# One hybrid decoder step on Trainium2: attention written as 16 steps, with each decode unit's stages apart and three shared banks

## The chip, the cores and the metric

The kernel runs on one core of a Trainium2 chip (trn2). The metric is the device time of one execution in microseconds; the median of the runs counts. On the core, TensorE (PE) multiplies, VectorE (DVE) and ScalarE (ACT) evict and do pointwise work, GpSimd (POOL) does little here, and SyncE (SP) issues the DMAs, in one queue.

## What is computed

```python
x = x + 0.5 * swiglu(rms_norm(x, f1n), f1g, f1u, f1d)
h = rms_norm(x, mix_n)
q, k, v, g, a_low, c_q, c_kv, k_pe_raw = jnp.split(h @ w_in, offsets, axis=-1)
o_gla, S = gla_mix(*gla_inputs(q, k, v, a_low, w_a_up, b_a))
y_gla = gla_output(o_gla, g, g_norm)
q_nope, q_pe, lat, k_pe = mla_project(c_q, c_kv, k_pe_raw, pos, q_norm, kv_norm, w_uq)
y_mla = mla_attend(q_nope, q_pe, lat, k_pe, w_uk, w_uv)
x = x + jnp.concatenate([y_gla, y_mla], axis=-1) @ w_out
x = x + 0.5 * swiglu(rms_norm(x, f2n), f2g, f2u, f2d)
```

There is one prompt of 1024 new tokens and eight samples of one new token each, with 4096 past tokens in a paged cache (latents of 128 and rotary keys of 64 a token). The width is 1024, the FFN's inner width 2816. Attention has four heads. For the prompt it is

```python
s = (jnp.einsum('bqhd,bkhd->bhqk', qn, k_nope)
     + jnp.einsum('bqhr,bkr->bhqk', qp, k_pe)).astype(jnp.float32) * MLA_SCALE
s = jnp.where(kpos[None, :] <= qpos[:, None], s, -jnp.inf)
p = jax.nn.softmax(s, axis=-1)
return jnp.einsum('bqhk,bkhd->bqhd', p.astype(v.dtype), v)
```

and for the samples the same over the cached latents, with the key and value weights absorbed into the queries and the output.

## The kernel before, in words

The program runs FFN1, the input projection, GLA, attention, the output projection with the mixer's sum, FFN2 and the last norm. All large products are three fp32r matmuls over a high and a low part of each operand; `split` (L83) makes the two parts, the high one on ACT (L84), the low one on DVE (L85), and `mm3` (L87, its matmul is L93) issues the three. The order of the instructions on each engine is left to the framework's scheduler, which takes what is ready by the order of the text; the text and the numbers of buffers in the pools are all that sets it.

*Pages.* Before decode can read the cache, 256 pairs of DMAs (`copies`, L188) bring its pages to contiguous DRAM (`kvd`, `ped`). `beside(n)` (L199) issues n of them: one after each of FFN1's seven products (L318, in `seven`), two at each tile of the input projection (L761), the rest ahead of GLA's levels (L1051).

*Decode.* There are 16 units (g, u), each of four samples and 512 past positions. `dec_unit` (L1191) does one in a row: fetch four latent tiles `kvt` and four key tiles `pet`; turn them with fp32 PE transposes, four to a bank (L1202 for `pet`, L1210 for `kvt`), copied to SBUF by DVE (`peT`, L1205) and ACT (`latT`, L1212); scores into one bank `dsc` (L1215, four matmuls of 512 columns, and L1218, eight of 256); softmax (L1188, L1189); four transposes of the probabilities `dpp` (L1224), a copy `dpT` (L1225), and 16 value matmuls (L1229). `dec_combine` adds the samples' own token and joins the eight units of a group. All these banks come from one pool of two, tag `pd` (the scores' bank from the same pool under a second tag).

*Prompt attention.* For each of two pairs of heads: the rotary queries `qs`, the values `v` (L1347 to L1349), then for each head the keys `k`, and four query blocks of 256. A block's `scores` makes the queries `q_h`, `q_l` and the score chunks `sc` (L1387 to L1393, three banks), the maximum, the exponentials `pp` (L1402) and their scaling (L1408). `outputs` of the block before turns `pp` (L1423, four transposes to a bank), splits it into `pT_h`, `pT_l` and multiplies by the values into `po` (one bank). Then `decode(1)` does one unit. Queries, keys, values and pp turns share two banks, tag `ps`. Two units are done ahead, during GLA.

After attention, `project` (from L1477) takes the GLA outputs `yraw`, split into `yg_h`, `yg_l`, the attention outputs `ym_h`, `ym_l`, and w_out (`raw`, split into `wh`, `wl`). The pool `raw` is shared by loads of all stages.

Of the kernel before, what the change touches and what calls it, by code (L numbers as in the profile page):

```python
# [67 lines left out]
def hybrid_step(ctx: ExitStack, tc: tile.TileContext, I, O, C):  # L68
# [226 lines left out]
    def seven(A, todo):  # L295
# [3 lines left out]
        for i in (1, 6, 2, 7, 5, 3, 4):  # L299
# [18 lines left out]
            beside()  # L318
# [517 lines left out]
    def rope(pool_, tag, dst, src, n, s):  # L836

        L = s.stop - s.start
        W = 512 if tag == "pp" else BL
        w = pool_.tile([P, 2 * W], F32, name="ropew", tag=tag, bufs=3 if tag == "pp" else 1)  # L840
# [101 lines left out]
    def levels(qr, st):  # L942
# [108 lines left out]
    beside(len(units) * 16)  # L1051
# [99 lines left out]

    early_raw = []
    for srcs in ([qnd[:, 0]], [qnd[:, 1]], [latd], [kpd, kpd]):
        raw = rawp.tile([P, SEQ], F32, name="raw", tag="raw")
        w = P // len(srcs)
        for i, src in enumerate(srcs):
            ld.dma_start(raw[i * w:(i + 1) * w], src)
# [4 lines left out]
    psD_cm, psd = pool("psD", 2, space=PSUM, side="right")  # L1162

    def dbank(name="pd"):
        return psd.tile([P, 512], F32, name=name, tag="pd")
# [6 lines left out]
    oT = ep.tile([P, NS, 32], F32, name="oT", bufs=1)  # L1172
    uv = ep.tile([P, 4, P], F32, name="uv", bufs=1)
    ld.dma_start(uv, w_uv)
    grp = {}

    def fetch(g, u):

        kvt = [ep.tile([P, J, P], F32, name="kvt", tag="kvt", bufs=6) for _ in range(4)]
        pet = [ep.tile([P, J, 64], F32, name="pet", tag="pet", bufs=6) for _ in range(4)]  # L1180
# [3 lines left out]
        return kvt, pet  # L1184
# [6 lines left out]
    def dec_unit(g, u):  # L1191

        if u == 0:
            grp[g] = (ep.tile([P, 3, NU + 1], F32, name="stat", tag="stat"), ep.tile([P, NU + 1, P], F32, name="oc", tag="oc", bufs=1))
        oc = grp[g][1]
        kvt, pet = fetch(g, u)
        sc = dbank("dsc")
        lt, pe = [], []
        for b2 in range(2):
            p = dbank()  # L1200
            for q in range(4):
                PE.transpose(p[:, q * P:(q + 1) * P],  # L1202
                             pet[2 * b2 + q // 2][:, 2 * (q % 2):2 * (q % 2) + 2, :].rearrange("p j c -> p (j c)"), ident)
            peT = ep.tile([P, 512], F32, name="peT", tag="peT")
            V.tensor_copy(peT, p)  # L1205
            pe += [peT[:, :256], peT[:, 256:]]
        for bi in range(4):
            p = dbank()
            for q in range(4):
                PE.transpose(p[:, q * P:(q + 1) * P], kvt[bi][:, 2 * (q % 2) + q // 2, :], ident)  # L1210
            lt.append(ep.tile([P, 512], F32, name="latT", tag="latT", bufs=4))
            S.activation(lt[bi], p, AF.Copy)  # L1212
        rows = [slice(32 * bi, 32 * bi + 32) for bi in range(4)]
        for bi in range(4):
            PE.matmul(sc[rows[bi], :], qlp[:, 4 * g + bi], lt[bi], start=True, stop=False)  # L1215
        for par in range(2):
            for bi in range(4):
                PE.matmul(sc[rows[bi], par * 256:par * 256 + 256], qpp[par][:, 4 * g + bi], pe[bi], start=False, stop=par == 1)  # L1218
        pp = ep.tile([P, 512], F32, name="dpp", tag="dpp")
        softmax(g, u, sc, 512, pp)  # L1220
        pT = ep.tile([P, J, P], F32, name="dpT", tag="dpT")
        p = dbank()
        for q in range(4):
            PE.transpose(p[:, q * P:(q + 1) * P], pp[:, q * P:(q + 1) * P], ident)  # L1224
        V.tensor_copy(pT.rearrange("p j q -> p (j q)"), p)  # L1225
        po = dbank()
# [3 lines left out]
        V.tensor_copy(oc[:, u], po[:, :P])  # L1230

    def dec_combine(g):
        stat, oc = grp[g]

        p = dbank()
        for bi in range(4):
            b = 4 * g + bi
            PE.matmul(p[32 * bi:32 * bi + 32, :NS], qlp[:, b], lat_s, start=True, stop=False)
            PE.matmul(p[32 * bi:32 * bi + 32, :NS], qpp[0][:64, b], kp_s, start=False, stop=True)
        sn = ep.tile([P, NS], F32, name="sn", tag="sn")  # L1240
        V.tensor_add(sn, p[:, :NS], newmask[:, g * NS:(g + 1) * NS])
        pn = ep.tile([P, NS], F32, name="pn", tag="pn")
        softmax(g, NU, sn, NS, pn)
        p = dbank()
        PE.transpose(p[:NS, :P], pn, ident)
        pnT = ep.tile([NS, P], F32, name="pnT", tag="pnT", bufs=1)
        V.tensor_copy(pnT, p[:NS, :P])
        p = dbank()
# [3 lines left out]
        cm = ep.tile([P, 4], F32, name="cm", tag="cm")  # L1252
        V.tensor_reduce(cm[:, 0:1], stat[:, 0, :], AX.X, OP.min)
        S.activation(stat[:, 2, :], stat[:, 0, :], AF.Exp, bias=cm[:, 0:1], scale=-1.0)
        V.tensor_mul(stat[:, 1, :], stat[:, 1, :], stat[:, 2, :])
        V.tensor_reduce(cm[:, 2:3], stat[:, 1, :], AX.X, OP.add)
        V.reciprocal(cm[:, 3:4], cm[:, 2:3])
        om = ep.tile([P, P], F32, name="om", tag="om", bufs=1)
        V.tensor_scalar_mul(om, oc[:, 0], stat[:, 2, 0:1])
        for u in range(1, NU + 1):  # L1260
            V.scalar_tensor_tensor(om, oc[:, u], stat[:, 2, u:u + 1], om, op0=OP.mult, op1=OP.add)
        V.tensor_scalar_mul(om, om, cm[:, 3:4])
        p = dbank()
# [428 lines left out]
```

## Time and profile before

| | |
|---|---|
| Median of three runs | 2098.72 us |
| Range of the runs | 2098.38 to 2100.55 us |
| Profiled execution, its time | 2100.9 us |
| Its span | 2099.1 us |
| PE busy | 2031.5 us (97%) |
| PE weight loads | 1915.6 us (91%) |
| DVE, ACT busy | 1471.5 us (70%), 838.0 us (40%) |
| Mean granted PE clock | 0.989 |

A row of the timeline gives the start, the duration, the engine and line, the operation with its output and inputs, and in brackets how long the engine was idle just before and what released it. A run of equal instructions is one row. The end of a matmul is modelled: the next one may start before it. "PE" is the matmul and "PEld" the load of its weights. The granted clock is given as a share of full speed, 1.00 being 2.4 GHz and 0.50 being 1.2 GHz.

### The profile page before, as it was taken

Reading aid. Unit: us, or ns where it says so; the run is one execution under the profiler, and the core shown is the slowest. Engines: PE = TensorE matmul, PEld = TensorE weight load, DVE = VectorE, ACT = ScalarE, POOL = GpSimd, SP = SyncE. Lnnn points to the kernel's source line nnn. Section 1 sums busy time; section 2 is a strip of 40 time slices with the busy share of each in tenths; the row PEclk is TensorE's granted clock in tenths of the full one; section 3 lists DMA queues with packets and bytes.
Section 4 is the critical chain, followed back from the end, with each engine's and each line's share of the span. In section 5 each row is a group of like instructions: output and inputs, shape, how many; then the busy total and the mean of one; then the engine's idle time right before and its main releaser. Section 6 shows DMA issues by size and latency. Waiting matters only on the chain.

```text
span 2099.1 us, 42793 instructions
## 1 busy us (share of the span) xinstructions
PE 2031.5 (97%) x16379; PEld 1915.6 (91%) x16379; DVE 1471.5 (70%) x2902; ACT 838.0 (40%) x1563; POOL 64.1 (3%) x95
## 2 busy tenths in 40 slices
PE   9999999999999999889899999999999999999997
PEld 8999999999999988888667777799999999999997
DVE  7876676675777865766565766488777778766775
ACT  7432322233344530436554644244323323333534
POOL 0000000000000000311000000000000000000000
PEclk9999999999999999999999999999999999999999
DMA  6444445467565623012443342744323233574352
GB/s 215 130 144 141 127 126 152 131 203 265 159 187 152 166 75 99 11 42 81 129 129 96 115 128 60 221 136 122 91 92 121 87 88 122 159 260 146 110 158 92
DMA packets 235837, 276.46 MB, mean 132 GB/s; under 512 B 27216, under 2 KB 186128, under 8 KB 235632
## 3 DMA queue, kind: packets, MB, share of 16 engines
q1 hardware_dynamic: 235632, 273.72, 42.7%
q8 instruction: 129, 2.11, 0.4%
q14 instruction: 76, 0.62, 0.1%
HBM read 214.34 MB, written 84.47 MB: 142 GB/s over the span
## 4 chain that ended last, share of the span: by engine, by line
PE 80%; DVE 8%; DMA 3%; ACT 3%; issue 2%; SPq 1%; POOL 1%; POOLq 0%; DVEq 0%; ACTq 0%
PE pp L93 34%; PE pp L448 20%; PE pw L93 6%; PE pr L93 4%; PE po L93 1%; PE pd L1210 1%; PE pw L1076 1%; PE dsc L1215 1%; DVE al L85 1%; PE pg L973 1%; PE ps L93 1%; PE dsc L1218 1%; PE ps L1423 1%; PE pd L1229 1%; DMA kvt<-kvd 1%
## 5 line engine op out<-in xcount | busy, mean ns | idle before, releaser
L93 PE MATMUL pp<-bh,ah 128*128 128x260 f32 (+1 forms) x2432 | 688.3, 283 | 9.7 <-DVE u L310 6.8
L93 PE MATMUL pp<-bl,ah 128*128 128x260 f32 (+1 forms) x2432 | 687.1, 283 | 1.8 <-DVE bl L85 1.8
L93 PE MATMUL pp<-bh,al 128*128 128x260 f32 (+1 forms) x2432 | 687.0, 283 | 0.6 <-DVE al L85 0.6
L93 PEld LDWEIGHTS pp<-bh,ah 128*128 128x128 f32 x2432 | 460.7, 189 | 12.1 <-DVE u L310 7.8
L93 PEld LDWEIGHTS pp<-bh,al 128*128 128x128 f32 x2432 | 462.1, 190 | 1.7 <-DVE al L85 1.7
L93 PEld LDWEIGHTS pp<-bl,ah 128*128 128x128 f32 x2432 | 459.8, 189 | 2.4 <-DVE bl L85 2.4
L448 PE MATMUL pp<-th,dl 128*128 128x256 f32 x1232 | 248.6, 283 | 1.2 <-DVE dl L85 1.2
L448 PE MATMUL pp<-tl,dh 128*128 128x256 f32 x1232 | 248.9, 283 | 0.1
L448 PE MATMUL pp<-th,dh 128*128 128x256 f32 (+1 forms) x1232 | 248.9, 283 | 0.0
L84 ACT ACTIVATE ah<-raw 128x512 fp32r<-128x512 f32 x208 | 128.8, 627 | 236.5 <-PE pp L93 219.0
L448 PEld LDWEIGHTS pp<-tl,dh 128*128 128x128 f32 x1232 | 190.0, 189 | 2.4 <-DVE tl L85 2.4
L448 PEld LDWEIGHTS pp<-th,dl 128*128 128x128 f32 x1232 | 189.9, 188 | 1.4 <-DVE dl L85 1.4
L448 PEld LDWEIGHTS pp<-th,dh 128*128 128x128 f32 x1232 | 190.8, 189 | 0.1
L84 ACT ACTIVATE dh<-a 128x1024 fp32r<-128x1024 f32 (+1 forms) x84 | 83.0, 988 | 253.9 <-PE pp L448 226.5
L85 DVE TENSOR_TENSOR al<-raw,ah 128x512 fp32r<-128x512 f32 x208 | 142.3, 688 | 48.7 <-ACT ah L84 47.2
L85 DVE TENSOR_TENSOR dl<-a,dh 128x1024 fp32r<-128x1024 f32 (+1 forms) x84 | 95.3, 1134 | 114.5 <-ACT dh L84 108.1
L84 ACT ACTIVATE ah<-sl 128x512 fp32r<-128x512 f32 x132 | 82.9, 630 | 201.0 <-PE pp L93 154.0
L93 PE MATMUL pw<-xh,wh 128*128 128x260 f32 (+4 forms) x320 | 101.1, 316 | 0.0
L93 PE MATMUL pw<-xh,wl 128*128 128x260 f32 (+4 forms) x320 | 100.5, 314 | 0.0
L93 PE MATMUL pw<-xl,wh 128*128 128x260 f32 (+4 forms) x320 | 100.1, 313 | 0.0
L85 DVE TENSOR_TENSOR tl<-traw,th 128x1032 fp32r<-128x1032 f32 (+1 forms) x84 | 95.6, 1138 | 3.8 <-ACT th L84 3.6
L85 DVE TENSOR_TENSOR al<-sl,ah 128x512 fp32r<-128x512 f32 x132 | 90.5, 688 | 10.9 <-ACT ah L84 8.1
(426 smaller groups left out, 3571.1 us busy)
## 6 DMA issues: line engine op xcount, KB each, us to landing
traw<-td SPq DMA_DIRECT2D x70, 516.0 KB
raw<-in_ffn_w_gate_dram SPq DMA_DIRECT2D x52, 512.0 KB
raw<-in_ffn_w_up_dram SPq DMA_DIRECT2D x52, 512.0 KB
a<-in_ffn_w_down_dram SPq DMA_DIRECT2D x40, 512.0 KB
kvd<-in_cache_kv_dram SPq DMA_DIRECT2D x256, 64.0 KB
kvt<-kvd SPq DMA_DIRECT2D x64, 256.0 KB
td<-q SPq DMA_DIRECT2D x22, 520.0 KB
td<-q SPq DMA_DIRECT2D x22, 512.0 KB
```

The source lines that it names most:

```text
L84: S.activation(out_h, src, AF.Copy)
L85: eng.tensor_sub(out_l, src, out_h)
L93: PE.matmul(ps, w_, x_, start=i == 0, stop=i == n - 1)
L448: PE.matmul(bank[c][m], w_[:, kk, ms], x_[:, kk, c * N[0]:c * N[0] + N[c]], start=first and j == 0 and (c == 1 or m % 2 == 0), stop=last a ...
L973: PE.matmul(p[:, t, c], kt[:, t, c * P:(c + 1) * P], qt[:, t, :, c * 64:(c + 1) * 64], start=True, stop=True)
L1076: PE.matmul(p[:n, :256], x_[:, k], w_[:, k % 4, :], start=i == 0, stop=i == 3 * KD - 1)
L1210: PE.transpose(p[:, q * P:(q + 1) * P], kvt[bi][:, 2 * (q % 2) + q // 2, :], ident)
L1215: PE.matmul(sc[rows[bi], :], qlp[:, 4 * g + bi], lt[bi], start=True, stop=False)
L1218: PE.matmul(sc[rows[bi], par * 256:par * 256 + 256], qpp[par][:, 4 * g + bi], pe[bi], start=False, stop=par == 1)
L1229: PE.matmul(po[rows[bi], :P], pT[:, (j % 2) * 2 + j // 2, rows[bi]], kvt[bi][:, j], start=j == 0, stop=j == J - 1)
L1423: PE.transpose(p[:, jj, qi * P:(qi + 1) * P], prs[qi][:, (j + jj) * P:(j + jj + 1) * P], ident)
```

## The change

1. Page copies: `seven` issues a copy after three of its seven products, the input projection four at each tile, GLA's `levels` four at each level, and the block of all remaining copies goes.
2. The rotary tables of the input projection's end and of attention come from the pool `raw`.
3. Attention is written as 16 steps, one for each head and block. `dec_unit` is cut into `fetch`, `turn`, `dec_scores`, `dec_softmax`, `dec_turn` and `dec_values`; `dec_own` and `dec_combine` are generators that go on a piece at a time (`tick`). In a step come the scores of the first query tile, the unit's scores, its softmax, the second query tile, the old block's pp turns, the unit's probability turn, the products, the values and the next unit's six turns (`t(0)` to `t(5)`) one at a time between these, and the next block's queries. Tiles are fetched two units ahead.
4. Banks: one for a unit's scores, its probability turns and its values (`sc_`); three, tag `ps`, for the unit's turns, pp turns, queries, keys, values and rotary queries. During GLA each of the two early units has one bank for turns and one for the rest.
5. Buffers: 11 `kvt` and 8 `pet` (6 and 6 before), `pp` as six tiles of 512 columns (three of 1024), `pT` two (three), `dpp`, `dpT` one (two).
6. `first_w`, one buffer of `raw`, is loaded ahead of the query and latent rows with the first heads' weights and the causal mask; `kp` is loaded later, inside attention; the value weights for the samples are loaded at the end, into a buffer of `raw`.

```diff
-            beside()
+            if i in (6, 7, 3):
+                beside()
...
-        beside(2)
+        beside(4)
...
+            beside(4)
...
-    beside(len(units) * 16)
...
+    first_w = rawp.tile([P, 1024], F32, name="first_w", tag="raw")
+    fw3 = [first_w[:, 256 * i:256 * i + 256].rearrange("p (k f) -> p k f", k=2) for i in range(3)]
+    for hh in range(2):
+        ld.dma_start(fw3[0][:, :, 64 * hh:64 * hh + 64], w_uq_[:, :, hh * 192 + P:hh * 192 + 192])
...
+
+    def dbank(tag="pt"):
+        if tag == "sc":
+            return unit_bank.tile([P, 512], F32, name="sc_", tag="sc_", bufs=1)
+        return psd.tile([P, 512], F32, name="pt", tag="ps") if psd is not unit_bank else psd.tile([P, 512], F32, name="pt", tag="pt", bufs=1)
...
+        kvt = [ep.tile([P, J, P], F32, name="kvt", tag="kvt", bufs=11) for _ in range(4)]
+        pet = [ep.tile([P, J, 64], F32, name="pet", tag="pet", bufs=8) for _ in range(4)]
...
+    def turn(g, u, i):
+
+        kvt, pet = got[g, u]
+        p = dbank()
+        for q in range(4):
+            src = kvt[i][:, 2 * (q % 2) + q // 2, :] if i < 4 else \
+                pet[2 * (i - 4) + q // 2][:, 2 * (q % 2):2 * (q % 2) + 2, :].rearrange("p j c -> p (j c)")
+            PE.transpose(p[:, q * P:(q + 1) * P], src, ident)
+        t_ = ep.tile([P, 512], F32, name="latT" if i < 4 else "peT", tag="latT" if i < 4 else "peT", bufs=4 if i < 4 else 2)
+        if i < 4:
+            S.activation(t_, p, AF.Copy)
+        else:
+            V.tensor_copy(t_, p)
+        turned[g, u, i] = t_
...
+    EARLY = 2
...
+    psD_cm, unit_bank = pool("psU", 1, space=PSUM, side="right")
+    ps_cm, ps = pool("psA_", 3, space=PSUM)
+    psd = ps
...
+    load_uqr(0)
+    split(qn_h[:, 0], qn_l[:, 0], early_raw[0])
+    split(qn_h[:, 1], qn_l[:, 1], early_raw[1])
+    rotary(0, 0, loads=True)
+    load_uk(0)
+    split(lat_h, lat_l, early_raw[2])
+    load_uq(0)
+    keys(0, 0)
+    queries(0, 0)
+    load_uv(0)
+    turn(*units[0], 0)
+    kraw_ = rawp.tile([P, SEQ], F32, name="raw", tag="raw")
+    for i in range(2):
+        ld.dma_start(kraw_[64 * i:64 * i + 64], kpd)
+    rotary(0, 0)
+    turn(*units[0], 4)
+    split(kp_h, kp_l, kraw_)
+    V.tensor_copy(identb, ident)
+    V.tensor_copy(causalb, first_w[:, 896:])
+    turn(*units[0], 1)
+    values(0, 0)
+    turn(*units[0], 5)
+    rotary(0, 1, loads=True)
+    values(0, 1)
+    turn(*units[0], 2)
+    turn(*units[0], 3)
+    rotary(0, 1)
...
+        s0 = scores(h, m, 0)
+        d(dec_scores)
+        maximum(*s0)
+        pr0 = exps(*s0, 0)
+        d(dec_softmax)
+        t(0)
+        s1 = scores(h, m, 1)
+        maximum(*s1)
+        factor(*s0)
+        if old:
+            old.turn(0)
+            old.part(0)
+            old.turn(1)
+            old.part(1)
+        pr1 = exps(*s1, 1)
+        tick()
+        t(4)
+        d(dec_turn)
+        if m == 3 and h == 1:
+            rotary(1, 0, loads=True)
+        t(1)
+        if old:
+            old.turn(2)
+            old.product(0)
+            old.part(2)
+        scale(pr0, s0[1])
+        factor(*s1)
+        tick()
+        if i and h % 2 == 0:
+            values(h // 2, 2 * m)
+        if m == 3 and h < 3:
+            load_uk(h + 1)
+            if h != 1:
+                load_uq(h + 1)
+        t(5)
+        if old:
+            old.turn(3)
+            old.product(1)
+            old.part(3)
+        if m == 3 and h == 1:
+            rotary(1, 0)
+        if unit and unit[1] == 0:
+            tick(20)
+        d(dec_values)
+        if new:
+            queries(*new)
+        scale(pr1, s1[1])
+        t(2)
...
+        if old:
+            old.product(2)
...
+        t(3)
+        if old:
+            old.product(3)
+            old.out()
...
+    uv = rawp.tile([P, 4, P], F32, name="uvr", tag="raw")
+    ld.dma_start(uv, w_uv)
+    old.turn(0)
...
```

**PE, a block in the steady part.** `pd<-ident,kvt` are turns of the decode tiles, `dsc` (after: `sc__`) the decode scores, `po` the prompt's value products, `ps<-ident,pp` the probability turns, `sc` the prompt's scores. Before, from the third last product of a block to the first scores of the next unit:

```order
L93 MATMUL po<-pT_l,v_h 128x256
L93 MATMUL po<-pT_h,v_l 128x256
L1210 MATMUL pd<-ident,kvt 128x128 x4
L93 MATMUL ps<-qn_h,uqh 128x256
L93 MATMUL ps<-qn_l,uqh 128x256
L1210 MATMUL pd<-ident,kvt 128x128 x8
L93 MATMUL ps<-qn_h,uql 128x256
L93 MATMUL ps<-qn_h,uqh 128x256
L1210 MATMUL pd<-ident,kvt 128x128 x4
L1215 MATMUL dsc<-latT,qlp 32x512 x4
L1218 MATMUL dsc<-peT,qpp_11185 32x256 x4
L1218 MATMUL dsc<-peT,qpp_11186 32x256 x4
```

The change, one unit's scores and what comes after:

```order
L1228 MATMUL sc__15509<-peT,qpp_10217 32x256 x4
L1228 MATMUL sc__15509<-peT,qpp_10218 32x256 x4
L1204 MATMUL pt<-ident,kvt 128x128 x4
L1452 MATMUL sc<-k_l,q_h 128x512
L1453 MATMUL sc<-k_h,q_l 128x512
L1454 MATMUL sc<-kp_h,qs_15198 128x512
L1455 MATMUL sc<-kp_l,qs_15198 128x512
L1457 LDWEIGHTS identb
L1457 MATMUL sc<-causalb,identb 128x128
L1502 MATMUL ps<-ident,pp 128x128 x4
L1204 MATMUL pt<-ident,pet 128x128 x4
L1239 MATMUL sc__15509<-ident,dpp 128x128 x4
```

Before, the four turns of the `kvt` tiles stand with two or three matmuls between them, right ahead of the scores that read them. After, the scores stand together, and the next unit's first `kvt` turn, a `pet` turn and a pp turn are apart, with the prompt's scores between the decode scores and the turn of their probabilities.

**PE, the front of attention.** Before, from the values of unit 1 on:

```order
L1229 MATMUL pd<-kvt,dpT 32x128 x16
L1202 MATMUL pd<-ident,pet 128x128 x4
L1347 MATMUL ps<-uv_h,lat_h 128x256
L1348 MATMUL ps<-uv_h,lat_l 128x256
L1349 MATMUL ps<-uv_l,lat_h 128x256
L1202 MATMUL pd<-ident,pet 128x128 x4
L1347 MATMUL ps<-uv_h,lat_h 128x256
L1348 MATMUL ps<-uv_h,lat_l 128x256
L1349 MATMUL ps<-uv_l,lat_h 128x256
L1210 MATMUL pd<-ident,kvt 128x128 x13
L1347 MATMUL ps<-uv_h,lat_h 128x256
```

The change, from the turns of unit 1 on:

```order
L1204 MATMUL pt<-ident,kvt 128x128 x12
L1239 MATMUL sc__15029<-ident,dpp 128x128 x4
L1204 MATMUL pt<-ident,kvt 128x128 x4
L1251 MATMUL sc__15029<-kvt,dpT 32x128 x16
L1204 MATMUL pt<-ident,pet 128x128 x4
L1223 MATMUL sc__15127<-latT,qlp 32x512 x4
L93 MATMUL ps<-qn_h,uqh 128x512
L1204 MATMUL pt<-ident,pet 128x128 x4
L1228 MATMUL sc__15127<-peT,qpp_10217 32x256 x2
L93 MATMUL ps<-qn_l,uqh 128x512
L93 MATMUL ps<-qn_h,uql 128x512
```

Before, the values L1347 to L1349 stand with the turns of unit 2 and no other work. After, unit 1's turns stand ahead of unit 0's `dpp` turn and values, the queries are laid among unit 1's scores, and the values have gone further back.

**ACT, the end of attention.** Before:

```order
L84 ACTIVATE yg_h_18428<-yraw_18444 128x1024
L84 ACTIVATE yg_h_18428<-yraw_18449 128x1024
L84 ACTIVATE pT_h_18339<-ps_18341 128x512
L84 ACTIVATE yg_h_18428<-yrs_18454 128x4x8
L84 ACTIVATE pT_h_18348<-ps_18350 128x512
L84 ACTIVATE wh_18463<-raw_18461 128x1024
L84 ACTIVATE ym_h_14924<-po_18357 128x256
L84 ACTIVATE wh_18498<-raw_18496 128x1024
```

The change:

```order
L84 ACTIVATE ym_h_14928<-ps_18357 128x8
L84 ACTIVATE wh_18457<-raw_18455 128x1024
L84 ACTIVATE pT_h_18376<-ps_18365 128x512
L84 ACTIVATE wh_18492<-raw_18490 128x1024
L84 ACTIVATE ym_h_14928<-po_18338 128x256
L84 ACTIVATE wh_18529<-raw_18527 128x1024
```

The first split of w_out (`wh`) has moved from behind the last `pT_h` to ahead of it, and one more w_out split stands ahead of that of the last prompt output, as before.

## Rows read from the trace of the kernel before

**Rows 1.** Page: busy time of PE; slices of its weight loads, in tenths.
```profile
PE 2031.5 (97%) x16379; PEld 1915.6 (91%) x16379; DVE 1471.5 (70%) x2902; ACT 838.0 (40%) x1563; POOL 64.1 (3%) x95
...
PEld 8999999999999988888667777799999999999997
```

**Rows 2.** Table by stage: us; busy PE, PEld, DVE, ACT, POOL; granted clock, DMA share.
```profile
1042.90:1313.80 270.90, 256.44 (x2177) 194.05 (x2173) 171.75 (x415) 142.25 (x335) 0.76 (x4) 0.97 0.36 109
1106.44:1237.62 131.18, 127.36 (x1129) 96.00 (x1132) 83.58 (x203) 68.91 (x164) 0.38 (x2) 1.00 0.37 116
...
1302.50:1309.30 6.80, 6.05 (x26) 5.36 (x27) 5.46 (x7) 5.02 (x8) 0.00 (x0) 0.50 0.43 113
```

**Rows 3.** Timeline of PE, one block of the steady part.
```profile
1144.14 1.04 PE L1210 MATMUL pd<-ident,kvt 128*128 128x128 f32 x8
1144.93 0.36 PE L1387 MATMUL sc<-k_h,q_h 128*128 128x256 f32 x1
1145.13 0.28 PE L1388 MATMUL sc<-k_l,q_h 128*128 128x256 f32 x1
1145.59 0.63 PE L1210 MATMUL pd<-ident,kvt 128*128 128x128 f32 x4 [0.18 <-DMA kvt<-kvd]
1146.15 1.43 PE L1215 MATMUL dsc<-latT,qlp 128*32 128x512 f32 x7
...
1148.81 0.38 PE L1389 MATMUL sc<-k_h,q_l 128*128 128x256 f32 x1
...
1150.09 0.39 PE L1390 MATMUL sc<-kp_h,qs 128*128 128x512 f32 x1
1150.32 0.39 PE L1391 MATMUL sc<-kp_l,qs 128*128 128x512 f32 x1
...
1152.18 1.08 PE L1229 MATMUL pd<-kvt,dpT 128*32 128x128 f32 x32
1153.08 0.20 PE L1238 MATMUL pd<-lat_s,qlp 128*32 128x8 f32 x2
...
1155.28 0.28 PE L93 MATMUL po<-pT_l,v_h 128*128 128x256 f32 x1
1155.40 0.28 PE L93 MATMUL po<-pT_h,v_l 128*128 128x256 f32 x1
1155.65 0.39 PE L93 MATMUL po<-pT_h,v_h 128*128 128x256 f32 x1
```

**Rows 4.** Listing by line of PE in the two heads (1106.44 to 1237.62).
```profile
L1210 PE MATMUL pd<-ident,kvt 128*128 128x128 f32 x128 | 19.1, 277 | 1.2 <-DMA kvt<-kvd 1.0
...
L1264 PE MATMUL pd<-ident,om 128*128 128x128 f32 x1 | 0.3, 271 | 0.0
```

**Rows 5.** PE's waits over the whole span: us in total, times, longest.
```profile
PE pp L93 <- DVE u L310: 6.8, 5, 2.7
...
PE pd L1229 <- DVE dpT L1225: 2.9, 1, 2.9
PE pr L93 <- DVE ym_l L85: 2.8, 1, 2.8
```

**Rows 6.** PE's waits from 1040 to 1314 us.
```profile
PE ps L1423 <- DVE pp L1408: 1.7, 1, 1.7
...
PE ps L1347 <- DVE v_l L85: 0.5, 1, 0.5
```

**Rows 7.** Timeline of all engines: a pp turn and its split; the tail.
```profile
1291.85 0.49 PE L1423 MATMUL ps<-ident,pp 128*128 128x128 f32 x3
...
1292.44 0.60 ACT L84 ACTIVATE pT_h<-ps 128x512 fp32r<-128x512 f32 x1 [2.02 <-PE ps L1423]
...
1293.07 0.69 DVE L85 TENSOR_TENSOR pT_l<-ps,pT_h 128x512 fp32r<-128x512 f32 x1 [0.44 <-ACT pT_h L84]
...
1308.34 0.60 ACT L84 ACTIVATE pT_h<-ps 128x512 fp32r<-128x512 f32 x1 [1.15 <-PE po L93]
...
1310.96 1.06 ACT L84 ACTIVATE wh<-raw 128x1024 fp32r<-128x1024 f32 x1 [2.03 <-PE po L93]
```

More of the change, by code (lines that the diff above doesn't have):

```diff
@@ L1189, in softmax, with dec_scores @@
         S.activation(pout[:, :n], sc[:, :n], AF.Exp, bias=stat[:, 0, u:u + 1], accum_out=stat[:, 1, u:u + 1])
-    def dec_unit(g, u):
+    def dec_scores(g, u):
         if u == 0:
[L1194 to L1206, printed above, removed]
-        for bi in range(4):
[L1208 to L1215, printed above, removed]
@@ L1219, in dec_unit @@
[L1219 to L1222, printed above, removed]
-        for q in range(4):
-            PE.transpose(p[:, q * P:(q + 1) * P], pp[:, q * P:(q + 1) * P], ident)
-        V.tensor_copy(pT.rearrange("p j q -> p (j q)"), p)
-        po = dbank()
+                o = 256 * (bi % 2)
+                PE.matmul(sc[rows[bi], par * 256:par * 256 + 256], qpp[par][:, 4 * g + bi], pe[bi // 2][:, o:o + 256],
+                          start=False, stop=par == 1)
@@ new lines, in values, with keys, queries @@
+    def values(t, j):
+        js, (uv_h, uv_l) = slice(j * P, (j + 1) * P), UV[t]
+        p = bank()[:, :256]
+        for i, (l_, r_) in enumerate(((lat_h, uv_h), (lat_l, uv_h), (lat_h, uv_l))):
+            PE.matmul(p, l_[:, js], r_, start=i == 0, stop=i == 2)
+        split(v_h[:, j], v_l[:, j], p)
+    def keys(h, b):
+        s = slice(b * 512, b * 512 + 512)
+        p = bank()
+        mm3(p, [(*UK[h], lat_h[:, s], lat_l[:, s])])
+        split(k_h[:, s], k_l[:, s], p)
+    def queries(h, m):
+        p = bank()[:, :256]
+        wt, s = W[h], QB[m]
+        mm3(p, [(wt[0][:, k], wt[1][:, k], qn_h[:, k, s], qn_l[:, k, s]) for k in range(2)])
+        Qm[h, m] = [ap_.tile([P, 256], F32R, name=f"q_{z}", tag=f"q_{z}") for z in "hl"]
+        split(*Qm[h, m], p)
@@ new lines, in hybrid_step, with d, t @@
+    V.tensor_copy(identb, ident)
[8 more added lines that the diff above has]
+    rotary(0, 1)
+    steps = [(h, m) for h in range(4) for m in range(4)]
+    old = None
+    for i, (h, m) in enumerate(steps):
+        unit, after, third = [units[j] if j < len(units) else None for j in range(i, i + 3)]
+        new = steps[i + 1] if i + 1 < len(steps) else None
+        def d(f, *a):
+            if unit:
+                f(*unit, *a)
+        def t(k):
+            if after:
+                turn(*after, k)
+        if third:
+            fetch(*third)
+        s0 = scores(h, m, 0)
[46 more added lines that the diff above has]
+        t(2)
+        if i and h % 2 == 0:
+            values(h // 2, 2 * m + 1)
+        tick()
+        if m == 1:
+            keys(h, 1)
+            if h == 1:
+                load_uqr(1)
+        if m == 2 and h == 1:
+            load_uq(2)
+            load_uv(1)
+        if old:
+            old.product(2)
+        if m == 3 and h < 3:
+            keys(h + 1, 0)
+            if h == 1:
+                rotary(1, 1, loads=True)
+        t(3)
+        if old:
+            old.product(3)
+            old.out()
+        if m == 3 and h == 1:
+            rotary(1, 1)
+        tick()
+        old = Values(h, m, (pr0, pr1))
+        if unit:
+            g, u = unit
+            if u == NU - 5:
+                slack.append(dec_own(g))
+            if u == NU - 1:
+                tick(20)
+                slack.append(dec_combine(g))
```

359 lines of the change are left out of this document (205 added, 154 removed).

## The prediction

> **What bounds the kernel now.** I read the page's engine list and its slices first. PE is busy for 2031.5 of 2099.1 us [rows 1], and its weight loads, which fill nine tenths of nearly every other slice, fill only six or seven in slices 20 to 24: that is attention. The table by stage then gives the attention stretch, from the last GLA matmul to the first output projection, 270.9 us, of which PE is recorded busy for 256.4, and inside it the steady part, two heads or eight blocks, 131.18 us or 16.4 us a block, PE recorded at 127.36 [rows 2]. Recorded idle is therefore 3.8 us there and 14.5 us in the whole stretch. DVE (83.6) and ACT (68.9) have slack on average, so no engine but PE can bound the steady part, unless by the order of single pieces.
>
> Is PE's 97% real? The timeline shows how fast PE goes when nothing holds it [rows 3]: eight transposes in 0.79 us (0.10 each), a unit's four and eight score matmuls in 2.66 us with one change of kind, a unit's 16 value matmuls in 0.9, a 512-column fp32r matmul in 0.23, a 256-column one in 0.12. The record of a matmul lasts 0.28 us, though the next can start 0.12 after it: a wait of up to 0.16 us hides inside "busy". It shows there: po matmuls 0.12 us apart, then one 0.25 later; and before the last turn of four transposes 0.46 us pass where 0.12 are needed, of which 0.18 is recorded as idle.
>
> So I count PE's own work in the two heads from the listing by line, 30 groups from the turns (L1210, 128) to the last single transpose, scores as L1387 in three widths [rows 4]. Transposes: 128 + 64 + 80 + 32 = 304 by 0.10 = 30. Decode scores 8 units by 2.55 = 20.4, decode values 8 by 0.9 = 7.2. 512-column fp32r: 60 scores, 12 rotary, 12 keys = 84 by 0.23 = 19.3. 384: 20 by about 0.175 (between the two rates) = 3.5. 256: 120 value products, 40 scores, 48 queries, 24 values = 232 by 0.12 = 27.8. Causal and the sample's own few, 3.5. The first fp32r matmul after an fp32 run starts about 0.1 us late (0.20 for 0.12 at 1144.93 to 1145.13, [rows 3]); some 65 such changes give 6. Together 117.7 of 131.2: **13.5 us are lost in eight blocks, 1.7 us a block**, 3.8 of it recorded.
>
> The Trainium skill (Perfetto Trace Analysis, Identifying the Most-Contended Engine) says that matmul busy time is a poor measure of headroom and that the weight loads' busy share is the good one. By the one measure the stretch could give at most 14.5 us, by the other 270.9 - 194.05 = 76.9 us [rows 2]; my count lies between, nearer the first.
>
> **The change, part by part.**
> *Page copies (seven, the input projection, levels, no catch-all).* It moves copies on SP's queue. The five long waits of FFN1 come from gate weights that stand behind copies, 6.8 us in all [rows 5]. In the orders of SP, each of FFN1's 52 gate and up loads has as many copies ahead of it as before, or up to three fewer, and from the 159th to the 221st copy the two orders keep within three of each other: 0, with 0 to -6.8 as bounds.
>
> *The steps.* Turns of the next unit are spread singly through the block, where before they stood three or four together in front of the scores that need them; the pet turns, the values and the probability turns are spread the same way, over three shared banks in place of two and two. PE's work is the same, and its changes between fp32 and fp32r runs fall from 259 to 221, half of which are into fp32r: 19 by 0.1 = -1.9. I laid the durations of rows along both orders (a turn, a 512-wide copy on ACT 0.6, a split 0.6 and 0.7 [rows 7]) and asked of each PE instruction how much other PE work stands between it and its producer. Of the steady waits about a third stay: after the change the next unit's turns have from 1 to 3 us of other work behind them, the dpp turns over 2 us behind the scores, the values over 2 behind those; what stays are products right behind a pT split, and a turn into a bank that a pT_l has just left. Fourteen blocks have a unit: 14 by 1.7 = 24; a third stays, 8; **-16**, bounds -24 and (if only recorded idle goes) 14 by 0.5 = -7.
>
> *The front.* Unit 0's values now stand 2.9 us behind their copy [rows 5], with PE idle. Now unit 1's turns stand between; but they go through one bank, each behind the copy of the one before: -1, bounds 0 and -2.9. Eight values in a row, each waiting on the split of an earlier one, one of them with 0.5 us recorded [rows 6], are spread over the first blocks; keys, queries and rotary work now fill the time around unit 1's scores: -4, bounds 0 and -6. New is that kp is loaded after the last y stores, and its split stands on ACT and DVE ahead of unit 1's exp: +1, bounds 0 and 2.
>
> *DVE.* Probabilities are scaled in two 512-wide pieces, one instruction more in each second query tile: some 0.15 us each, in a stretch where DVE is 63% busy; the cover is PE's, and if DVE were late at pT_l it would be a part of the third that stays: 0.
>
> *The tail.* After the last scores there is nothing to fill with: idle of 1.7 and 2.8 us is recorded [rows 5, 6], and the clock is at half (0.50 for 6.80 us, [rows 2]). In the change ACT's queue has a w_out split ahead of the last pT_h, where it stood behind, and the value weights take a raw buffer among the y loads, so that the w_out load waits for one y split more. ACT was idle 2.03 us before that w_out split began at 1310.96, 2.6 us after the last pT_h's 1308.34 [rows 7]: if w_out lands no sooner, pT_h waits for 2.6 + 1.06 = 3.7 us. As the y splits come sooner and so the load too, I take +2, bounds -1 and +5.
>
> Sum: -1.9 - 16 - 1 - 4 + 1 + 2 = -19.9. The profiled run took 2100.9 us (the table of times), 0.1% above the median of 2098.72: 2100.9 - 19.9 = 2081, and 2.2 lower for a median run: 2079. Since the waits that I count as gone leave room for smaller ones that I do not see, I say **2080 us**. Likeliest case 2070 to 2090.
>
> **Rivals.**
> *Only the recorded idle goes.* What I call hidden waiting is then PE's own time (weight loads that do not overlap, slower first matmuls). For it: in the steady part PE's rows fill 97%. Against it: the 0.25 us starts among po matmuls. Gain: 14 blocks by 0.5, the front's 3, less the tail's 2: 8 us; 2098.7 - 8 = 2091. Chance 0.16.
>
> *Three shared banks too few (slower).* Before, turns had their own two banks, and pp turns, queries, keys and values two others. Now all of them pass three in turn: a block has 6 turns, 2.5 pp turns, 1 query, 1 value, and about 1.3 others, some 11.8 uses. A bank is held from the first transpose to the end of the split: 1291.85 to 1293.76, 1.9 us for pp turns [rows 7], about 1.2 for a turn. Three banks in blocks of 15.3 us allow 3 by 15.3 / 11.8 = 3.9 us each. It decides when mean holding passes that, as when ACT's in-order queue has an exp that waits for scores ahead of the copy. Each 0.1 us above costs 11.8 by 0.1 / 3 = 0.4 us a block. At 4.4 us of holding it takes 2 us a block, 32 in all: 2080 + 32 = 2112. Against: two banks at the steady part gave a granted clock of 1.00 and 1.7 us of loss only. The Trainium skill (TensorE: Matmul & The Clock Gate, A second HAM failure mode: psum-queue depth-cycling) warns that cycling banks leaves small pauses that let the clock swing; no swing shows in the steady rows. If pauses at a block's end did what those of the tail do (half clock, [rows 2]), a stretch of 3.4 us a block would cost 1.7 us by 16, 27 us. Chance of this rival 0.12.
>
> *The time moves from PE's waits to the queues.* Spread pieces mean that ACT and DVE get each copy behind another exp or reduce; they are in order, and the same 1.7 us is lost at other places: 2095 to 2101. Against it: both have over 30% free. Chance 0.08.
>
> **How the numbers follow.** The forecast has 0.60, the first rival 0.16, the slower one 0.12, the third 0.08; 0.04 is for more than the forecast, where the weight loads' room shows. A measurement of this kernel can tell about 0.2%, 4 us, from no change; so the forecast, the first rival and the 0.04 are faster, 0.80; the third is the same, 0.08; slower is 0.12. The range goes from 2066 (the steps' whole 24 us and a free tail: 2080 - 8 - 6) to 2097 (the first rival with a tail of 5 and some of the third).
>
> **What would show it.** Right: the two-head stretch takes 122 us or less with PE's rows unchanged in number; the turns (L1204) and decode score rows follow others without idle; the wait for dpT at the front is gone; the tail is longer by 1 to 3 us, with PE waiting for pT_h behind wh. FFN1's five waits stay at about 7 us. Wrong: the two heads take 128 us or more with less idle (first rival), waits of turns or of pp turns for a bank (WAR on latT, pT_l) or a granted clock below 1.00 in the steady part (second), or more waiting for ACT and DVE copies in place of the old ones (third).

## The result, and the profile after

The change takes 2078.6 us (median of four runs, 2077.4 to 2080.8), the kernel before in the same runs 2098.55. The ratio is 0.9901, with a 95% interval from 0.9886 to 0.9916: faster by about 1%, 20 us. The prediction was 2080, its range 2066 to 2097.

First the table by stage: span; busy PE, PEld, DVE, ACT, POOL; granted clock, DMA share, GB/s. I cut attention into three pieces by marks that both traces have: the *front*, from the last GLA turn to the first block's first causal matmul (the one that adds the causal mask); the *steps*, from there to the last causal matmul; and the *tail*, from there to the first output projection. Before:

```profile
1038.00:1075.25 37.25, 31.20 (x237) 21.33 (x236) 23.27 (x47) 20.43 (x43) 0.00 (x0) 0.86 0.47 144
1075.25:1298.01 222.76, 217.01 (x1915) 165.08 (x1914) 140.30 (x352) 112.11 (x273) 0.76 (x4) 1.00 0.34 104
1298.01:1313.76 15.75, 10.22 (x58) 8.99 (x57) 11.99 (x23) 10.63 (x21) 0.00 (x0) 0.78 0.36 96
```

The change, the same pieces, and FFN2's long middle for comparison:

```profile
1035.00:1057.74 22.74, 19.29 (x185) 13.16 (x186) 17.03 (x34) 13.85 (x28) 0.00 (x0) 1.00 0.79 229
1057.74:1272.17 214.43, 211.57 (x1966) 166.27 (x1964) 150.00 (x380) 118.98 (x290) 0.66 (x3) 1.00 0.34 103
1272.17:1289.94 17.77, 14.12 (x74) 12.68 (x74) 14.79 (x28) 11.48 (x22) 0.20 (x1) 0.67 0.52 141
...
1385.70:1832.80 447.10, 446.94 (x3760) 446.44 (x3761) 351.01 (x701) 154.43 (x270) 1.97 (x2) 1.00 0.37 113
```

All three pieces together go from 275.8 to 254.9 us: **attention gives 20.8 us, the whole gain**. The stages outside moved by up to 2.4 us each, either way. Recorded idle in attention (span less PE busy) falls from 17.3 to 10.0, by 7.3; the other 13.5 us came out of time in which PE is recorded busy. PE's recorded matmuls there are no fewer (2210 and 2225, the three pieces' counts added up; a few records are missing in each). So that was waiting hidden in the busy rows, and at the two ends, where the clock was below 1.00, also matmuls at half clock.

Where it was hidden, the waits of the weight loads show. In the rows they start ahead of their matmuls, so an operand that is late shows as idle time of the loads first. Before, the steps:

```profile
PEld dsc L1215 <- ACT latT L1212: 7.4, 21, 0.7
PEld pd L1210 <- ACT latT L1212: 4.7, 11, 1.0
PEld sc L1387 <- ACT q_h L84: 4.7, 9, 0.8
...
PEld po L93 <- ACT pT_h L84: 2.7, 8, 0.9
...
PEld pd L1210 <- DVE peT L1205: 1.9, 8, 0.3
...
PEld pd L1229 <- DVE dpT L1225: 1.1, 3, 0.4
```

The change, the steps:

```profile
PEld pt L1204 <- issue: 5.8, 13, 0.8
...
PEld sc L1451 <- ACT latT L1207: 1.7, 2, 0.8
PEld pt L1204 <- ACT latT L1207: 1.6, 3, 0.8
...
PEld pt L1204 <- DVE pT_l L85: 1.2, 5, 0.2
...
PEld sc L1452 <- DVE k_l L85: 1.0, 4, 0.2
PEld po L1519 <- DVE pT_l L85: 0.9, 4, 0.4
```

The six before sum to 22.5 us, the five after with a named releaser to 6.4; all the named ones together fell from some 29 us to 13. Rows marked "issue", in which the loads wait for nothing that the profile shows, rose from some 14 to 23 us and are not counted here. A load's wait is not yet a loss of PE, which may still have matmuls to do: the sums fell by 16 us, the steps' span by 8.3. The largest, 7.4 us at 21 places, is the decode scores waiting for `latT` copies, the last one above all; 0.5 us at one place is left of it. What it did to PE is seen in the timeline. Of a steady unit in the change:

```profile
1130.37 1.07 PE L1223 MATMUL sc__16340<-latT,qlp 128*32 128x512 f32 x8
1131.25 1.05 PE L1228 MATMUL sc__16340<-peT,qpp 128*32 128x256 f32 x16
1132.23 0.66 PE L1204 MATMUL pt<-ident,kvt 128*128 128x128 f32 x4
```

The twelve score matmuls (24 records, two for each) take 1.86 us, from 1130.37 to 1132.23. Before they took 2.66, from 1146.15 to 1148.81 [rows 3], with no idle recorded. ACT's row shows what they waited for, the last copy, which ended at 1146.92, 0.8 us after the first score had begun; the weight loads' row shows the wait, 0.67 us:

```profile
1146.32 0.60 ACT L1212 ACTIVATE latT<-pd 128x512 f32<-128x512 f32 x1 [0.39 <-PE pd L1210]
...
1146.96 0.11 PEld L1215 LDWEIGHTS dsc<-latT,qlp 128*32 128x32 f32 x1 [0.67 <-ACT latT L1212]
```

In the steps before, nine of the thirteen units have their scores in a row, in 2.4 to 2.7 us; in the change ten of fourteen, each in 1.86. Between the first causal matmuls of heads 0 and 2, 129.0 us have become 116.8.

### The profile page after: what moved, and what is told of

It reads as the page before. It is cut to its first block, busy times and chain, and to the rows that moved or that the text cites. A ratio compares the mean times of both kernels' runs of the same rounds, so it can differ in the third digit from the quotient of the medians.

```text
span 2076.8 us, 42809 instructions
## 1 busy us (share of the span) xinstructions
PE 2015.7 (97%) x16379; PEld 1906.8 (92%) x16379; DVE 1473.1 (71%) x2918; ACT 840.7 (40%) x1565; POOL 66.1 (3%) x95
## 4 chain that ended last, share of the span: by engine, by line
PE 79%; DVE 9%; DMA 4%; ACT 3%; issue 3%; SPq 1%; POOL 1%; POOLq 0%; ACTq 0%; DVEq 0%
PE pp L93 34%; PE pp L449 19%; PE pw L93 6%; PE pr L93 4%; PE pt L1204 2%; DMA raw<-in_ffn_w_gate_dram 1%; PE po L1519 1%; DVE al L85 1%; PE pw L1077 1%; PE ps L93 1%; DVE qt L971 1%; DMA xraw<-x2d 1%; PE pg L975 1%; PE ps L1502 1%; DVE q L382 1%
## 5 line engine op out<-in xcount | busy, mean ns | idle before, releaser
L93 PE MATMUL pp<-bh,ah 128*128 128x260 f32 (+1 forms) x2432 | 686.1, 282 | 12.1 <-DVE u L310 10.4
L93 PEld LDWEIGHTS pp<-bh,ah 128*128 128x128 f32 x2432 | 458.9, 189 | 14.6 <-DVE u L310 11.6
L85 DVE TENSOR_TENSOR al<-sl,ah 128x512 fp32r<-128x512 f32 x132 | 90.1, 684 | 12.5 <-ACT ah L84 10.2
```

Of the source, the lines that this page charges most:

```text
L85: eng.tensor_sub(out_l, src, out_h)
L93: PE.matmul(ps, w_, x_, start=i == 0, stop=i == n - 1)
```

## The experiments

Each was timed against the kernel before on its own chip, so ratios are compared, and the three pieces of attention. Those repeat far better than the total: the change itself, run again (e7), has steps of 214.56 against 214.43 us, while the stages ahead of attention differ by 7 us between the two executions.

| run | ratio to before (95%) | front | steps | tail | sum, us |
|---|---|---|---|---|---|
| before | 1 | 37.25 | 222.76 | 15.75 | 275.8 |
| the change | 0.9901 (0.9886 to 0.9916) | 22.74 | 214.43 | 17.77 | 254.9 |
| e1 copies back | 0.9898 (0.9882 to 0.9915) | 22.69 | 214.46 | 17.78 | 254.9 |
| e2 turns together | 0.9897 (0.9877 to 0.9916) | 22.69 | 217.75 | 17.76 | 258.2 |
| e3 two banks | 1.0060 (1.0043 to 1.0077) | 24.43 | 244.64 | 21.45 | 290.5 |
| e4 tail's weights early | 0.9937 (0.9917 to 0.9958) | 25.64 | 214.37 | 17.83 | 257.8 |
| e5 banks of before | 0.9941 (0.9918 to 0.9964) | 22.79 | 217.17 | 18.37 | 258.3 |
| e6 new banks in before | 1.0185 (1.0168 to 1.0202) | 33.22 | 252.62 | 22.57 | 308.4 |
| e7 the change again | 0.9907 (0.9891 to 0.9924) | 22.71 | 214.56 | 16.75 | 254.0 |
| e8 copies alone in before | 1.0003 (0.9989 to 1.0017) | 36.98 | 222.91 | 15.66 | 275.6 |
| e9 turns in their own step | 0.9986 (0.9969 to 1.0004) | 22.68 | 231.91 | 17.69 | 272.3 |
| e10 early slot loaded late | 0.9889 (0.9861 to 0.9917) | 22.72 | 214.50 | 17.78 | 255.0 |
| e11 one unit ahead | 0.9895 (0.9870 to 0.9920) | 18.81 | 220.44 | 16.23 | 255.5 |
| e12 turns ahead, in before | 1.0019 (1.0007 to 1.0030) | 42.95 | 223.75 | 15.36 | 282.1 |

**e1, the copies put back** (in the change).

```diff
-            if i in (6, 7, 3):
-                beside()
+            beside()
...
-        beside(4)
+        beside(2)
...
-            beside(4)
...
+    beside(len(units) * 16)
```

> The change with its first part undone: a page copy after each of FFN1's products, two at a tile of the input projection, the rest in a block ahead of GLA. The theory of the order (the gain comes from decode and prompt pieces laid apart in attention): attention keeps its 255 us within 1 us; FFN1's wait for u (10.4 us with the change, 6.8 before) goes back to about 7, so 1 to 3.5 us faster than the change in FFN1, and GLA gives up to 2.4 us back: 2076 to 2080 us. The rival that the copies carry part of the gain: 2082 us or more.

**e8, the copies alone** (the same lines the other way round, in the kernel before).

> The kernel before with the change's first part alone (page copies after three products, four at a tile and at each GLA level). The prediction took 0 for it: 2096 to 2101 us, the five long waits of FFN1 unchanged at 7 to 10 us. If the copies carry part of the gain: 2094 us or less, with the input projection or GLA 2 us shorter.

Neither moves the time: 0.9898 beside the change's 0.9907 and 0.9901, and 1.0003 beside 1. Attention is the same to 0.2 us. FFN1's wait for `u`, 6.8 before and 10.4 after, was 9.5 in e1 and 9.1 in e8, and 9.7 in the change run again: it varies by 3 us between executions and does not follow the copies. The forecast of 0 for this part stands; e1's expectation of 1 to 3.5 us was wrong in taking 6.8 and 10.4 for properties of the kernels.

**e2, the six turns together, still a step ahead.**

```diff
-        t(0)
...
-        t(4)
...
-        t(3)
+        for k_ in (4, 5, 0, 1, 2, 3):
+            t(k_)
```

> The change with the next unit's six turns called together near the end of a step, in place of one at a time through it; banks, buffers, fetches and the rest stay. Theory of the order: each turn waits for a bank whose copy has just begun, the scores for the last copy, and the fp32r work has less to stand between; 8 to 16 us of the 21 that attention gained come back: 2086 to 2095 us, and most of it not as recorded idle. Rival, banks and buffers make the gain: within 3 us of the change, 2076 to 2082 us.

A miss: 3.3 us in the steps, not 8 to 16, and nothing that the total can tell. In its trace the turns do stand together, by twos, at the end of a block; but the rest of the prompt's scores comes between the last turn (started at 1156.2) and the unit's scores (1158.6), and most units still take 1.86 us. That turns stand singly is not what carries the gain.

**e9, each unit's turns in its own step.** All six calls `t(k)` and the six ahead of the steps go, and stand ahead of the scores:

```diff
+        for k_ in (4, 5, 0, 1, 2, 3):
+            d(turn, k_)
         d(dec_scores)
```

> The change with each unit's six turns called in its own step, right ahead of its scores, as before, in place of one step earlier; fetches two units ahead, banks and the rest stay. So far the attention stage (last GLA turn to first output projection) repeats within 1 us over executions: 275.8 before, 255 in the change, 258.4 with the turns together but a step ahead. If the gain in the steps comes from having the turns a step ahead of the scores: 262 to 268 us of attention, 8 to 13 above the change, 2086 to 2094 us in all. If the distance of turn and score does not matter (the other stages laid apart make it): 255 to 260 us, 2079 to 2085 us.

17.5 us come back in the steps, beyond the 8 to 13 expected; the total is that of before (0.9986). That is more than the 8.3 us by which the change shortened the steps: with the new order and banks, turns in their own step are worse than they were before (231.9 us with 14 units in the steps, 222.8 with 13, and a unit costs 6.0 in e11). So e9 shows that the new order needs its turns a step ahead, and not what share of the gain they make. It keeps the fetches two units ahead and their buffers, so these alone do not make the gain either. Its timeline shows the mechanism, a unit's scores behind its turns:

```profile
1151.65 1.91 PE L1223 MATMUL sc__16513<-latT,qlp 128*32 128x512 f32 x6
1153.49 0.51 PE L1452 MATMUL sc<-k_l,q_h 128*128 128x512 f32 x1
1153.93 0.62 PE L1223 MATMUL sc__16513<-latT,qlp 128*32 128x512 f32 x1
...
1154.39 1.45 PE L1228 MATMUL sc__16513<-peT,qpp 128*32 128x256 f32 x10
1155.77 0.50 PE L1453 MATMUL sc<-k_h,q_l 128*128 128x512 f32 x1
```

The scores take from 1151.65 to 1155.77, 4.1 us with one prompt matmul among them, where 1.86 do. ACT has put a prompt exponential between the copies that they read:

```profile
1150.13 1.18 ACT L1207 ACTIVATE latT<-pt 128x512 f32<-128x512 f32 x2 [3.77 <-PE pt L1204]
1151.20 0.68 ACT L1472 ACTIVATE pp<-sc,mx 128x512 f32<-128x512 f32 x1
...
1151.87 1.08 ACT L1207 ACTIVATE latT<-pt 128x512 f32<-128x512 f32 x2
```

No idle is recorded in any of PE's rows there. In all the steps e9 has 3.7 us of recorded idle (231.91 less 228.22), the change 2.9.

**e12, turns a step ahead in the kernel before**, and nothing else of the order (two `pT` in place of three, and more `kvt` and `pet`, for the tiles in flight).

```diff
-    def dec_unit(g, u):
...
+    def dec_prepare(g, u):
...
             dec_unit(g, u)
+            if i_ + 1 < len(units):
+                dec_prepare(*units[i_ + 1])
```

> The kernel before with one thing of the change: each unit's tiles are fetched and turned right behind the unit ahead of it, so that its scores come a block later (eight kvt and seven pet buffers, pT two in place of three to make room); banks, the order of the prompt's work, values in a row and the loads as before. If turns a step ahead are enough for the gain in the steps: from the first block's last prompt score to the last one 208 to 216 us (222.8 before, 214.4 in the change, 231.9 in the change with the turns in their own step), and 2086 to 2094 us in all, the front's gain being left out. If it needs the rest of the order or the banks too: 218 us or more, 2094 us and above.

Turns a step ahead are not enough: 223.75 us of steps, 1.0 more than before, and a longer front, since one more unit's turns (those of unit 3) moved into it. The waits went to other links. PE's, from the end of GLA to the output projection:

```profile
PE pd L1231 <- ACT dpp L1189: 7.3, 7, 3.5
PE pd L1236 <- DVE dpT L1232: 3.5, 3, 2.9
```

These are 10.8 us of idle at two links that had 0.8 (`dpp`) and 2.9 (`dpT`, [rows 5]) before: a unit's probability turn stands too close behind its scores, and its values behind their copy. But 8.2 of the 10.8 stand ahead of the steps and 2.6 in them (0.4 before). In the steps the weight loads say more:

```profile
PEld sc L1398 <- ACT q_h L84: 5.7, 11, 1.8
...
PEld pd L1231 <- ACT dpp L1189: 3.8, 6, 1.1
...
PEld dsc L1222 <- ACT latT L1210: 1.7, 6, 0.4
```

The scores' wait for `latT` did fall, from 7.4 to 1.7 us; that of the probability turns rose from 0.6 to 3.8, and that for `q_h` from 4.7 to 5.7. Part of it may be the smaller `pT`; that was not tried apart.

**e3, two shared banks; e5, the banks of before; e6, the new banks in before.** In e3, `pool("psA_", 2, ...)`. In e5 the unit has two banks, and its scores, probability turn and values one each in turn; the prompt has two. In e6 the kernel before gets one bank for the unit and three shared.

```diff
-    ps_cm, ps = pool("psA_", 3, space=PSUM)
+    ps_cm, ps = pool("psA_", 2, space=PSUM)
```

> The change with two shared banks in place of three, one bank left unused. The prediction's holding sum: 11.8 uses a block of about 14.6 us, so two banks allow 2.5 us each against 1.2 to 1.9 held; a pp turn that waits for its split behind other work goes beyond that: 0.2 to 0.6 us a block, 3 to 10 us, 2082 to 2089 us. Rival, that the third bank carries the gain: 15 us or more back, 2094 us and above. If banks do not matter at all: 2077 to 2080 us.

> The change's text with the banks of before: two for the unit (scores, probability turn and values each take one of their own, in turn with the six turns) and two for the prompt's pp turns, queries, keys and values. If the order alone makes the gain: 2078 to 2086 us. If the banks alone make it: 2095 to 2100 us, as before. If each needs the other: in between or above, 2086 to 2110 us, with PE waiting for banks (turns behind latT, peT) in the steady blocks.

> The kernel before, its text and order of calls, with the change's banks: one for a unit's scores, probability turn and values, three shared by turns, pp turns, queries, keys, values. If the banks alone make the gain: 2080 to 2086 us. If the order alone makes it: 2094 to 2100 us, as before. If each needs the other: 2088 to 2105 us, the decode unit now bound in one bank, its next scores waiting for its values' copy.

The steps of the three, in that order, one line from the table by stage of each:

```profile
1058.98:1303.62 244.64, 233.54 (x1978) 173.27 (x1975) 154.38 (x383) 122.69 (x292) 0.52 (x3) 0.98 0.30 89
```

```profile
1064.89:1282.06 217.17, 211.51 (x1972) 167.04 (x1970) 154.98 (x387) 124.09 (x296) 0.72 (x4) 1.00 0.34 103
```

```profile
1073.02:1325.64 252.62, 231.41 (x1971) 177.18 (x1969) 145.98 (x356) 114.56 (x279) 0.69 (x4) 0.97 0.30 93
```

The order with the old banks keeps 17.5 of the 20.8 us of attention (275.8 to 258.3); the new banks with the old order cost 32.6. So the order makes the gain, and the banks add 3.4 us to it in attention, but only with it. The totals put more on the banks: e5's median is 7.2 us above that of e7, the change on the same chip (2088.0, from runs between 2081.3 and 2091.9, and 2080.9); what lies outside attention there is not explained. In e6 recorded idle alone is 21.2 us of the steps, and PE's largest wait there is a turn behind DVE's `om` (5.2 us); how much the one bank for all of a unit's stages adds was not tried apart. And the layout has no reserve: e3 loses 30 us in the steps with one shared bank less, against 3 to 10 expected. The other parts of the change (`pp` in six tiles, the rotary tables in `raw`, `kp` loaded later) were not tried apart.

**e4, the samples' value weights loaded early**, into a buffer of their own (and ten `kvt`).

```diff
+    uv = ymp.tile([P, 4, P], F32, name="uv")
...
-    uv = rawp.tile([P, 4, P], F32, name="uvr", tag="raw")
```

> The change with the samples' value weights loaded early into a buffer of their own, so that they take no raw buffer among the y loads at the end (ten kvt buffers in place of eleven, to make room). If the buffer is what lengthened the tail: from the last prompt scores to the first output projection 15.8 to 16.5 us instead of 17.8, 2076.5 to 2078 us in all. If the tail's length is the place of the w_out split in ACT's queue or PE's chain alone: 17.5 to 18 us, and 2078 to 2080 us.

The tail stays at 17.83 us, so the raw buffer is not what lengthened it. The steps are as in the change with ten `kvt` as with eleven; 3 us are lost at the front, with a new wait of 2.2 us for a `peT` copy of the first unit; whether that is the eleventh buffer or the load's place is open. The total lost more, 5.9 us against e1, which is as fast as the change, on the same chip (2086.4 and 2080.5); where the rest lies is open too.

**e10, the early slot loaded late** (the block that loads `first_w` moved to just ahead of `load_uqr(0)`).

> The change with the buffer of early weights loaded inside attention, ahead of the first rotary queries, in place of ahead of the query rows. The stretch from the last GLA turn to the first block's last prompt score took 37.3 us before and 22.7 in the change, with a granted clock of 0.86 and 1.00. If the early weights are what keeps PE fed and its clock up there: 27 to 33 us and a clock below 0.95, 2083 to 2092 us in all. If the order of the text alone does it (unit 1's turns, keys and queries laid among each other): 22 to 25 us, 2078 to 2084 us.

The front is the same to 0.02 us. The early weights do nothing here. What is left is the order of the text, and with it the banks: e6, with the old order and the new banks, has a front of 33.22 us, 4.0 shorter than before. e5, the new order with the old banks, has 22.79.

**e11, one unit ahead of the steps** (`EARLY = 1`).

> The change with one decode unit ahead of the steps in place of two, so that 15 of 16 steps have a unit and the last but one too. The front loses unit 1's serial work (6 us of own work, about 6 us of waits), step 15 has filler for its 2 us of pp waits. If idle PE at the two ends is what is left to gain: 3 to 8 us less attention, 247 to 252 us, 2071 to 2078 us in all. If the front then waits for its loads instead, and the tail's half clock (11.7 us at 0.5) stays: 253 to 257 us, 2077 to 2083 us.

The front is 3.9 us and the tail 1.5 us shorter, the steps 6.0 longer, since they hold a unit more: no gain. A unit costs 6.0 us in the steps, where leaving it out of the two ends saves 5.4.

**e7, the change again.**

> The change itself, unaltered, on the chip of these runs: 0.990 of before, 2077 to 2083 us. It sets the scale for the small differences: stage by stage its attention takes 255 us from the last GLA turn to the first output projection, and FFN1, projection and GLA should repeat within 1 us if their small changes (FFN1 +1, GLA -2.4) are the kernel's and not the execution's.

```profile
1064.51:1279.07 214.56, 211.67 (x1966) 166.27 (x1964) 150.10 (x380) 119.16 (x290) 0.67 (x3) 1.00 0.34 103
1279.07:1295.82 16.75, 12.54 (x74) 11.06 (x74) 13.40 (x27) 11.43 (x22) 0.20 (x1) 0.81 0.48 130
```

Attention repeats to 1 us; the tail is 1.0 shorter, with its clock at 0.81 in place of 0.67. The clock does not explain that: e4 and e9 have 0.81 and 0.89 there, and tails of 17.83 and 17.69 us. The other stages repeat less well: the first down projection of FFN1 starts 4.3 us later. No run beat the change by more than its interval.

## Why the prediction was right, point by point

The total was right, 2079 by the sum and 2080 forecast against 2078.6, and so was the place: attention, by waits hidden in PE's busy time. The first rival is refuted: of 20.8 us, recorded idle gave 7.3. But two terms of the sum missed by some 4.6 us each, one too large and one too small, and a third was right for a wrong reason: that the sum came out within 1 us was luck.

*The steps, -16 and -1.9 for changes of kind: by my count -11.5 and about -2.* I counted PE's own work again, by the prediction's rates, over all three pieces; this is an estimate. Before: 230 us of work and 45.5 lost (front 14.6, steps 21.7, tail 9.2). After: 229.6 and 25.3 (5.9, 10.2, 9.2). The steps' span fell by less than 11.5, by 8.3, since between these marks the change has the scores of 14 units and the kernel before those of 13. The failing step is "a third stays". One rate under it was wrong: the 2.55 us for a unit's scores were taken as work, and hold 0.7 us of waiting for `latT`. With 1.86 the steps' loss is 30.7 us before and some 20 now, so nearer two thirds stay. The nine or ten units in a row by 0.7 make 6 to 7 us, and the loads' list has 7.4 for the copy ahead of the scores: more than half of what went, as far as the rows show. How the rest divides among the other waits of the list (`q_h`, `pT_h`, banks) is not shown. And "spread singly" was the wrong half of the reason: e2 shows 3.3 us for that; without the turns a step ahead the steps lose 17.5 (e9), and with them alone nothing is gained (e12).

*The front, -4 and -1 and +1: by my count -8.7 of lost time.* The term that I left out is the clock. In the front it was 0.86 on average before and is 1.00 now. With levels of 0.50 and 1.00 that is 28% of 37.25 us at half speed, some 10 us. A row of the front before, from a stretch with a granted clock of 0.51 (1039.60 to 1046.50), shows what that does: a unit's value matmuls, after 2.86 us of idle, take 1.94 us, where in the steps they take 1.08 [rows 3]:

```profile
1041.05 1.94 PE L1229 MATMUL pd<-kvt,dpT 128*32 128x128 f32 x32 [2.86 <-DVE dpT L1225]
```

If all of PE's work in these 10 us took twice as long, it cost some 5 us; that is an estimate, and an upper one. e8, with the order and banks of before, speaks against the whole of it: its clock was lower (0.82) and its front no longer (36.98). So what else shortened the front is open. I had the rows of a half clock for the tail [rows 2], and did not price the same at the front, where the waits of 2.9 and 0.5 us [rows 5, 6] stood next to it. The wait for `dpT` is 0.8 us now, not gone.

*The tail, +2: measured +2.0.* Right in size, not in reason. `wh` does stand ahead of the last `pT_h`, but ACT began `wh` at 1285.75 and `pT_h` at 1286.70, right behind it: less than one `wh` of 1.05, not 3.7.

```profile
1285.75 1.05 ACT L84 ACTIVATE wh<-raw 128x1024 fp32r<-128x1024 f32 x1
1286.70 0.58 ACT L84 ACTIVATE pT_h<-ps 128x512 fp32r<-128x512 f32 x1
...
1286.83 1.23 DVE L85 TENSOR_TENSOR wl<-raw,wh 128x1024 fp32r<-128x1024 f32 x1 [0.68 <-ACT wh L84]
1287.97 0.68 DVE L85 TENSOR_TENSOR pT_l<-ps,pT_h 128x512 fp32r<-128x512 f32 x1
```

The w_out split does hold the last products up, but on DVE: `pT_h` is done at 1287.28, `pT_l` starts behind `wl` at 1287.97, and PE is idle for 0.79 us until it is there. The loss by my count is 9.2 us in both kernels. Some 2 us more of PE's own work came into the tail (6.6 to 8.6); recorded idle fell from 5.5 to 3.7, and half-clock time rose instead, from 6.9 us (0.78 on average of 15.75) to 11.7 (0.67 of 17.77). That does not set the tail's length: with 0.81 it was 16.75 in e7 and 17.83 in e4.

*The banks.* The second rival did not come: in the steps the clock was 1.00, and the turns' weight loads waited 1.2 us in all for a bank behind a `pT_l` and 1.6 us behind a `latT`. Its sum was wrong all the same. By mean holding, two banks would have allowed 2.6 us for each use (2 by 15.3 / 11.8), more than the 1.9 of a pp turn, and e3 would have cost little. It cost 30 us. A likely reason, not shown apart, is that uses come in bursts, so that one waits for an earlier one's copy whatever the mean: in e3 the turns' loads wait 3.8 us behind a `pT_l` (1.2 in the change). The Trainium skill (TensorE: Matmul & The Clock Gate, A second HAM failure mode: psum-queue depth-cycling) warns of a clock that swings where banks are cycled. No swing shows in the change's steps, where the clock was 1.00 with three shared banks; in e3 and e6 it was 0.98 and 0.97, but with 11 and 21 us of recorded idle, so the runs cannot tell the one from the other.

*The copies* were rightly 0. *The measure of headroom*: the Trainium skill (Perfetto Trace Analysis, Identifying the Most-Contended Engine) puts the weight loads' busy share, beside the share of peak arithmetic, in place of the matmuls' busy share. Here the loads' share promised too much: PEld filled 73% of the two heads [rows 2], and fills 78% of the steps now (166.27 of 214.43), with some 20 us left by my count. The loads' *waits* were the better row, for where to look: 22.5 us of them had a named copy or split before, in steps in which I count some 31 us as lost and PE's own rows show 5.7 of idle. The two slips of reading that I find in the prediction change nothing: the loads are at six or seven tenths up to slice 26, not 24, and the range's lower end takes 6 us for a free tail where the tail's own bounds (+2 and -1) give 3.

## What to carry to other kernels

Where an engine reads as 97% busy and its rows are pipelined, list the waits of the queue that runs ahead of it (here the weight loads): a wait of about a matmul's recorded length, like the 0.7 us here, may show nowhere else. Take the list as a map of places, not as a sum of gains. Put the work that feeds a chain (transpose, copy, product) one step ahead of its reader, and let the next link have other work behind it as well: one link alone only moves the wait (e12). Bank layout and order go together; test each with the other's old form before keeping it, since the layout that gains 3 us here costs 33 with the old order.

## What was not expected of the hardware

The steps of attention repeat to 0.2 us over five executions of nearly the same order (the change, e1, e4, e7, e10: 214.37 to 214.56), on several chips, while the start of attention moves by up to 7 us between the change and its repetition: a difference of a few us is to be read from the piece, not from the total. The twelve decode score matmuls, each over 32 columns of the array, take 1.86 us in a row, though the trace gives each of the four wider ones two records of 0.60 us: the eight stand within 1.07 us, so they overlap, and a wait of 0.7 us among them left no trace in PE's own rows.
